# A row-wise NaN-ignoring maximum on one core: every second load of the middle tiles issued from ScalarE's queue instead of SyncE's

## The chip, the core and the metric

The kernel runs on one core of a Trainium2 chip. A core has engines with instruction streams of their own. Four of them take part here: ScalarE (ACT), GpSimd (POOL), VectorE (DVE) and SyncE (SP). SP only issues transfers. The transfers themselves are carried out by 16 DMA engines, which move data between the device's main memory (HBM) and the core's on-chip memory (SBUF, 128 partitions). An engine that issues a load does not wait for it; the load raises a semaphore when it has landed, and whoever needs the data waits on that.

The metric is the device time of one execution in microseconds (us), as the median over the runs shown.

## The reference

The input is a float32 array of 32 x 2048 x 2048. About a tenth of its elements are NaN. The result is the maximum of each row of 2048 over the elements that are not NaN:

```python
def reference(x, axis):          # axis is -1
    return np.nanmax(x, axis=axis).astype(np.float32)
```

That is 65,536 rows, 537 MB read and 0.26 MB written.

## The kernel before

**Tiles.** The rows are spread over the 128 partitions, 512 rows for each. What a partition has is cut into 74 tiles, listed in `TILES`. Lengths there are counted in quarters of a row (`Q` = 512 elements). An ordinary tile has 28 quarters, seven rows for each partition, 7,168 KB in all. An entry has three lists: how the tile is loaded, how its passes are cut, and how its reductions are cut. `([28], [7, 9, 12], [16, 12])` is one load of 28 quarters, three pieces of 7, 9 and 12 quarters, and two reductions over 16 and 12 quarters. The first tile is small; tiles 2 to 62 (counted from one) are loaded whole; the last twelve tiles come in several loads.

**Passes.** Each piece goes through three engines, all in place in the tile's buffer `xt`:
- ACT's key pass (`e_key = act(...)`) reads the upper half-word of every element and writes a 16-bit key to a buffer `kt`. The pass maps NaN below every number.
- POOL's pass turns the key back into a half-word and writes it over the upper half of the element. A negative number in the list of pieces gives that pass to ACT instead (`release()`). In five of the middle tiles, the 9th, 17th, 25th, 33rd and 41st, this is the last piece: they are cut `[9, 12, -7]`.
- DVE reduces finished stretches of the tile to row maxima (`tensor_reduce`).

ACT's third key pass of an ordinary tile also waits for POOL's first pass, since key buffers are shared.

**Buffers and order.** There are `BUFS` = 3 tile buffers. The load into a buffer waits for the last reduction of the tile that was there before, three tiles back (`free[...]`). The program is written out as one long list without loops on the chip: `Order.add` emits an instruction on an engine, puts the waits that are still needed in front of it, and returns an event for others to wait on. Each engine executes its list in order. All loads are issued by SP, in the order of the tiles, on SP's DMA queue. They use `LANES` = 14 semaphores in turn; a load also waits until the earlier one of its lane has landed.

In the profile all of ACT's passes have line 226, POOL's 236, reductions 243, and the issues of loads 307. The loop over pieces is where the change is made: `number` is already counted up there, so `number - 1` is the index, from zero, of the tile in hand.

```python
xt, before = xts[number % BUFS], free[number % BUFS]
number += 1
...
free[(number - 1) % BUFS] = after[-1:]
```

Of the kernel before, what the change touches and what calls it, by code (L numbers as in the profile page):

```python
# [10 lines left out]
Q = D // 4  # L11
# [38 lines left out]
GROUPS = [TILES[i : i + 15] for i in range(0, 60, 15)] + [TILES[60:73], TILES[73:]]  # L50
# [7 lines left out]
BUFS = 3  # L58
# [4 lines left out]
LEAD = 128  # L63

LANES = 14

# [9 lines left out]
def total(pieces):  # L78
    return sum(sum(map(abs, p)) if isinstance(p, tuple) else abs(p) for p in pieces)
# [93 lines left out]
def kernel(  # L173
# [15 lines left out]
    nc = tc.nc  # L189
    P = nc.NUM_PARTITIONS  # L190
# [9 lines left out]
    xr = x.bitcast(i32).flatten_outer_dims()  # L200
    R = xr.shape[0]
    of = out.bitcast(i32).flatten_outer_dims().rearrange("r c -> (r c)")
    rows = [sum(sum(loads) for loads, _, _ in g) * Q // D for g in GROUPS]
# [9 lines left out]
    xts = [sing.tile([P, WIDE * D], i32, name=f"xt{i}") for i in range(BUFS)]  # L213
# [5 lines left out]
    with tc.tile_critical():  # L219
        order = Order(nc)  # L220
# [51 lines left out]
        free = [[] for _ in range(BUFS)]  # L272
# [3 lines left out]
        def last(uses):  # L276

            return list({back: e for back, _, e in sorted(uses, key=lambda u: u[1])}.values())

        key = 0  # L280
        used = KEYS
        number = 0
        lanes = [[] for _ in range(LANES)]
        turn = 0
        stores = []
# [2 lines left out]
        r0 = 0  # L288
        for gi, (s, g) in enumerate(zip(rows, GROUPS)):
            xg = xr[r0 : r0 + P * s].rearrange("(p s) d -> p (s d)", p=P)  # L290
# [4 lines left out]
            base = 0  # L295
            for loads, pieces, reds in g:
                assert sum(loads) == total(pieces) == sum(reds)
                xt, before = xts[number % BUFS], free[number % BUFS]
                number += 1
                landed = []  # L300
                at = 0
                for c in loads:
                    c *= Q
                    e = order.add(
                        "sp",
                        nc.sync,
                        lambda: nc.sync.dma_start(  # L307
                            out=xt[:, at : at + c], in_=xg[:, base + at : base + at + c]
                        ),
                        before + lanes[turn],  # L310
                        lane=f"load{turn}",
                        step=16,
                    )
                    lanes[turn] = [e]
                    turn = (turn + 1) % LANES
                    landed.append((at, at + c, e))
                    at += c
                clean = []
                after = []
                at = done = 0  # L320
                reds = [n * Q for n in reds]
                part = []
                held = []
                pairs = {}
                if number not in APART:
                    pairs = joints(pieces, [n // Q for n in reds])
                flat = sum((p if isinstance(p, tuple) else (p,) for p in pieces), ())
                half = {}
                piece = 0

                def cleaned(a, b, k, i, e):

                    nonlocal clock
                    clock += 1
                    both = [(a, b, k, flat[i] < 0, clock)]
                    if i in pairs:
                        if pairs[i] not in half:
                            half[pairs[i]] = both
                            return
                        both += half.pop(pairs[i])  # L340
                    for a, b, k, back, when in both:
                        kfree[k].append((back, when, e))
                        clean.append((a, b, e))

                def name(i):
                    return f"pair{number}_{pairs[i][0]}" if i in pairs else None

                def release():
                    for a, b, k, kp, e, i in held:
                        e = act(  # L350
                            [e],
                            name(i),
                            out=xt[:, a:b].bitcast(i16)[:, 1::2],
                            in_=kp,
                            func=ACT.Copy,
                            bias=float(TOP),
                            scale=-1.0,
                        )
                        cleaned(a, b, k, i, e)
                    held.clear()  # L360

                for parts in pieces:
                    parts = parts if isinstance(parts, tuple) else (parts,)
                    c = int(sum(map(abs, parts))) * Q
                    here = [l for a, b, l in landed if a < at + c and b > at]
                    kold = []
                    if used + c > KEYS:
                        key = (key + 1) % NKEYS
                        used = 0
                        kold, kfree[key] = last(kfree[key]), []  # L370
                        assert all(k != key for q in half.values() for _, _, k, _, _ in q)
                        if at + c == sum(loads) * Q:

                            kold = kold + last(kfree[(key + 1) % NKEYS])
                    e_key = act(
                        here + kold,
                        out=kts[key][:, used : used + c],
                        in_=xt[:, at : at + c].bitcast(i16)[:, 1::2],
                        func=ACT.Prelu,
                        bias=EDGE,  # L380
                        scale=-1.0,
                        alpha=float(TOP - LOW) / (EDGE - NAN),
                    )
                    release()
                    for c in parts:
                        back, wait, c = c < 0, isinstance(c, float), int(abs(c)) * Q
                        kp = kts[key][:, used : used + c]
                        used += c
                        to = xt[:, at : at + c].bitcast(i16)[:, 1::2]
                        at += c  # L390
                        if back:
                            held.append((at - c, at, key, kp, e_key, piece))
                            if not wait or at == sum(loads) * Q:
                                release()
                        else:
                            e = pool(
                                [e_key],
                                name(piece),
                                out=to,
                                in0=kp,  # L400
                                scalar1=-1.0,
                                scalar2=float(TOP),
                                op0=ALU.mult,
                                op1=ALU.add,
                            )
                            cleaned(at - c, at, key, piece, e)
                        piece += 1
                        open_ = [h[0] for h in held] + [p[0] for q in half.values() for p in q]
                        while reds and done + reds[0] <= min([at] + open_):
                            n = reds.pop(0)  # L410


                            lo = done - 1 if done % D else done
                            done += n
                            row = (base + lo) // D
                            if done % D:
                                m, to = 1, xt[:, done - 1 : done].bitcast(f32)
                            else:
                                m = max(n // D, 1)
                                to = acc[:, row : row + m]  # L420
                            e = dve(
                                [e for a, b, e in clean if b > lo and a < done] + part,
                                nc.vector.tensor_reduce,
                                out=to,
                                in_=xt[:, lo:done]
                                .bitcast(f32)
                                .rearrange("p (c d) -> p c d", c=m),
                                axis=mybir.AxisListType.X,
                                op=ALU.max,
                            )  # L430
                            part = [e] if done % D else []
                            after.append(e)
                free[(number - 1) % BUFS] = after[-1:]
                base += at
# [16 lines left out]
        for (og, bits), e in zip(stores, ready):  # L451
# [5 lines left out]
                lane="store",  # L457
                step=16,
# [39 lines left out]
```

## Time and profile before

| what | value |
|---|---|
| median of 3 runs | 1252.92 us (1252.90 to 1252.95) |
| the profiled execution's own time | 1252.86 us |
| its span in the profile | 1251.1 us |
| DVE busy | 1110.8 us, 89% |
| ACT busy | 965.5 us, 77% |
| POOL busy | 1168.4 us, 93% |
| moved by DMA | 537.20 MB, mean 429 GB/s |

The span is what the profiler sees of the program, from its first instruction to its last; the time of the execution has a little more around it. Busy times of the engines overlap, so they do not add up. A line of the timeline has the start in the span, the duration, the engine and line, what is written from what, and in brackets how long the engine had been idle before and who released it; several instructions in a row are put together (x2), and gaps inside such a group are counted in its duration.

### The profile page before, as it was taken

How to read it: one execution, taken by the hardware profiler on the slowest of the kernel's cores; microseconds unless marked ns; L12 is line 12 of the kernel's file. 1: busy time of each engine (PE TensorE's matmuls, PEld its weight loads, DVE VectorE, ACT ScalarE, POOL GpSimd, SP SyncE). 2: the span in 40 equal slices, each digit the busy share in tenths (PEclk: the TensorE clock that was granted, in tenths of full speed). 3: DMA queues.
4: the chain of work that ended last, by engine and by line, in shares of the span. 5: the costliest groups of instructions: out<-in, count | busy, mean ns of one | idle time of the engine just before them, and what ended most of it. 6: DMA issues, size and time to landing. Idle time of an engine off the chain costs nothing.

```text
span 1251.1 us, 893 instructions
## 1 busy us (share of the span) xinstructions
DVE 1110.8 (89%) x181; ACT 965.5 (77%) x273; POOL 1168.4 (93%) x242
## 2 busy tenths in 40 slices
DVE  0888989888889888898988888998888899999999
ACT  3777887778777877788777877777777778999997
POOL 2999989998999899998999899999999999989998
DMA  9999999999999999999999999999999999999997
GB/s 415 438 416 436 440 440 436 415 440 440 438 433 420 440 440 436 433 422 440 440 436 433 422 440 438 438 433 422 440 438 437 435 422 436 427 438 428 429 428 298
DMA packets 15992, 537.20 MB, mean 429 GB/s; under 512 B 2545, under 2 KB 2545, under 8 KB 3569
## 3 DMA queue, kind: packets, MB, share of 16 engines
q1 hardware_dynamic: 15984, 537.14, 99.4%
q14 instruction: 8, 0.06, 0.0%
HBM read 536.87 MB, written 0.26 MB: 429 GB/s over the span
## 4 chain that ended last, share of the span: by engine, by line
DMA 40%; DVE 29%; POOL 22%; ACT 9%; issue 1%; SPq 0%
DMA xt<-in_x_dram 40%; DVE acc L243 29%; POOL xt L236 22%; ACT kt L226 8%; ACT xt L226 1%; SPq L307 0%; DVE none L249 0%; DVE acc L263 0%; SPq L493 0%; SPq L219 0%
## 5 line engine op out<-in xcount | busy, mean ns | idle before, releaser
L236 POOL TENSOR_SCALAR xt<-kt 128x3584 int16<-128x3584 uint16 (+11 forms) x236 | 1167.3, 4946 | 77.9 <-ACT kt L226 64.0
L243 DVE TENSOR_REDUCE acc<-xt 128x3 f32<-128x6144 f32 (+4 forms) x175 | 1107.6, 6379 | 136.6 <-POOL xt L236 129.1
L226 ACT ACTIVATE kt<-xt 128x3584 uint16<-128x3584 int16 (+9 forms) x247 | 913.3, 3734 | 278.3 <-DMA xt<-in_x_dram 258.3
L226 ACT ACTIVATE xt<-kt 128x512 int16<-128x512 uint16 (+6 forms) x24 | 52.9, 2202 | 0.7
L226 ACT ACT_TABLE_LOAD x1 | 1.3, 1283 | 0.9 <-SPq L219 0.9
L243 DVE TENSOR_REDUCE xt<-xt 128x1 f32<-128x1536 f32 x1 | 1.7, 1739 | 0.0
L269 DVE MEMSET scalars<- 128x1 f32 x1 | 0.1, 59 | 1.0 <-SPq L219 1.0
L249 DVE TENSOR_SCALAR none<-acc 128x414 int32<-128x414 f32 (+1 forms) x2 | 0.8, 381 | 0.1
L263 DVE TENSOR_TENSOR acc<-acc,none 128x414 int32<-128x414 int32 (+1 forms) x2 | 0.7, 374 | 0.1
L249 POOL TENSOR_SCALAR late<-acc 128x91 int32<-128x91 f32 x1 | 0.5, 547 | 0.1
L263 POOL TENSOR_TENSOR acc<-acc,late 128x91 int32<-128x91 int32 x1 | 0.3, 342 | 0.1
L479 POOL MEMSET const-float32-0.0<- 128x1 f32 x1 | 0.1, 98 | 0.2 <-issue 0.2
L226 ACT ACTIVATE scalars<-scalars 128x1 f32<-128x1 f32 x1 | 0.2, 203 | 0.0
L479 POOL MEMSET const-bfloat16-1.0<- 128x1 bf16 x1 | 0.1, 101 | 0.0
L479 POOL MEMSET const-uint8-127<- 128x1 uint8 x1 | 0.1, 101 | 0.0
L479 POOL MEMSET const-float32-1.0<- 128x1 f32 x1 | 0.1, 98 | 0.0
## 6 DMA issues: line engine op xcount, KB each, us to landing
xt<-in_x_dram SPq DMA_DIRECT2D x61, 7168.0 KB, 22.6
xt<-in_x_dram SPq DMA_DIRECT2D x2, 5120.0 KB, 17.5
xt<-in_x_dram SPq DMA_DIRECT2D x3, 2816.0 KB, 22.6
xt<-in_x_dram SPq DMA_DIRECT2D x4, 2048.0 KB, 22.3
xt<-in_x_dram SPq DMA_DIRECT2D x5, 1536.0 KB, 29.1
xt<-in_x_dram SPq DMA_DIRECT2D x2, 3584.0 KB, 24.7
xt<-in_x_dram SPq DMA_DIRECT2D x6, 1024.0 KB, 26.8
xt<-in_x_dram SPq DMA_DIRECT2D x3, 1792.0 KB, 30.0
```

The lines of the kernel that those rows point to most:

```text
L226: lambda: nc.scalar.activation(**kw),
L236: lambda: nc.gpsimd.tensor_scalar(**kw),
L243: return order.add("dve", nc.vector, lambda: do(**kw), deps)
L249: lambda: engine.tensor_scalar(out=none, in0=acc, scalar1=NONE, scalar2=float(0x00800000), op0=ALU.is_equal, op1=ALU.mult,),
L263: lambda: engine.tensor_tensor(out=bits, in0=bits, in1=none, op=op),
L269: e_warm = order.add("dve", nc.vector, lambda: nc.vector.memset(warm, 1.0), [])
L479: nc = _bacc.Bacc("TRN2", target_bir_lowering=False, num_devices=1)
```

## The change

A set of tiles `BESIDE` is defined: those with index 4, 6, ... 58 from zero, the 5th to the 59th, 28 in all. The load of such a tile is no longer issued by SP. ACT issues it, on ACT's own DMA queue. In ACT's list it stands two tiles earlier in the program: behind the last key pass of the tile two back (all these tiles have three key passes), and ahead of that tile's own copy by ACT where the last piece is negative. It waits for the same event as before, the last reduction of the tile that had the buffer, and in principle for the earlier load of its lane, of which ACT has three of its own. The table `places`, filled ahead of the loop, says where in the input each tile lies. When the loop comes to such a tile, it takes the event of the load already issued and gives SP nothing to issue. The loads of the other tiles, and of all from the 60th on, stay on SP.

```diff
+BESIDE = range(4, 60, 2)
+BLANES = 3
...
+        blanes = [[] for _ in range(BLANES)]
+        bturn = 0
+        ahead = {}
+        places = {}
+        at = r0 = 0
+        for s, g in zip(rows, GROUPS):
+            xg = xr[r0 : r0 + P * s].rearrange("(p s) d -> p (s d)", p=P)
+            r0 += P * s
+            base = 0
+            for loads, _, _ in g:
+                places[at] = (xg, base, sum(loads) * Q)
+                base += sum(loads) * Q
+                at += 1
...
+                if number - 1 in ahead:
+                    landed.append((0, sum(loads) * Q, ahead.pop(number - 1)))
+                    loads = []
+                size = total(pieces) * Q
                 for c in loads:
...
-                for parts in pieces:
+                for step, parts in enumerate(pieces):
...
                     release()
+                    if number + 1 in BESIDE and step == len(pieces) - 1:
+                        xa, ba, na = places[number + 1]
+                        ahead[number + 1] = order.add(
+                            "act",
+                            nc.scalar,
+                            lambda: nc.scalar.dma_start(
+                                out=xts[(number + 1) % BUFS][:, :na], in_=xa[:, ba : ba + na]
+                            ),
+                            free[(number + 1) % BUFS] + blanes[bturn],
+                            lane=f"beside{bturn}",
+                            step=16,
+                        )
+                        blanes[bturn] = [ahead[number + 1]]
+                        bturn = (bturn + 1) % BLANES
```

The remaining lines of the diff put `size` where `sum(loads) * Q` stood, since `loads` is emptied for these tiles.

More of the change, by code (lines that the diff above doesn't have):

```diff
@@ L371 @@
                         assert all(k != key for q in half.values() for _, _, k, _, _ in q)
-                        if at + c == sum(loads) * Q:
+                        if at + c == size:
                             kold = kold + last(kfree[(key + 1) % NKEYS])
@@ L392 @@
                             held.append((at - c, at, key, kp, e_key, piece))
-                            if not wait or at == sum(loads) * Q:
+                            if not wait or at == size:
                                 release()
```

## The prediction

> **What bounds the kernel now.** I read the page first, for the engines' shares and the transfers.
>
> ```profile
> DVE 1110.8 (89%) x181; ACT 965.5 (77%) x273; POOL 1168.4 (93%) x242
> DMA packets 15992, 537.20 MB, mean 429 GB/s; under 512 B 2545, under 2 KB 2545, under 8 KB 3569
> q1 hardware_dynamic: 15984, 537.14, 99.4%
> xt<-in_x_dram SPq DMA_DIRECT2D x61, 7168.0 KB, 22.6
> ```
>
> The transfers use 99.4% of what the 16 DMA engines have in the span, all on one queue; POOL, the busiest engine, has 93%. A 7,168 KB load lands 22.6 us after its issue. Next, the table by stretches (length, busy time with instruction counts of DVE, ACT and POOL, clock, DMA share, GB/s):
>
> ```profile
> 20.00:500.00 480.00, 415.96 (x55) 364.07 (x88) 451.33 (x81) 1.00 1.00 434
> 500.00:1000.00 500.00, 447.66 (x60) 378.11 (x92) 481.33 (x88) 1.00 1.00 434
> ```
>
> In the whole middle, where the change lies, the DMA share is 1.00 and the rate is 434 GB/s in both halves. At that rate one tile, 7.34 MB, takes 16.91 us. The view of the transfers in a stretch of that length shows what they are made of:
>
> ```profile
> DMA packets 144, 7.34 MB, mean 434 GB/s; under 512 B 16, under 2 KB 16, under 8 KB 16
> q1 hardware_dynamic: 144, 7.34, 100.3%
> ```
>
> 128 large packets and 16 tiny ones: for each DMA engine eight data packets of 16.91 / 8 = 2.11 us and one small closing packet. Then the waits and the timeline:
>
> ```profile
> ACT kt L226 <- DMA xt<-in_x_dram: 258.3, 69, 15.0
> SPq L307 <- DVE acc L243: 1155.7, 71, 37.8
> ```
>
> ```profile
> 78.12 6.54 DVE L243 TENSOR_REDUCE acc<-xt 128x3 f32<-128x6144 f32 x1
> 81.02 5.32 ACT L226 ACTIVATE kt<-xt 128x6144 uint16<-128x6144 int16 x1 [0.38 <-POOL xt L236]
> 84.69 17.26 SPq L307 DMA_DIRECT2D xt<-in_x_dram  x2
> 90.42 7.12 ACT L226 ACTIVATE kt<-xt 128x3584 uint16<-128x3584 int16 x2 [4.08 <-DMA xt<-in_x_dram]
> 93.69 16.74 POOL L236 TENSOR_SCALAR xt<-kt 128x3584 int16<-128x3584 uint16 x3 [0.16 <-ACT kt L226]
> 97.92 5.32 ACT L226 ACTIVATE kt<-xt 128x6144 uint16<-128x6144 int16 x1 [0.38 <-POOL xt L236]
> 103.34 15.14 DVE L243 TENSOR_REDUCE acc<-xt 128x4 f32<-128x8192 f32 x2 [1.75 <-POOL xt L236]
> 107.36 7.12 ACT L226 ACTIVATE kt<-xt 128x3584 uint16<-128x3584 int16 x2 [4.11 <-DMA xt<-in_x_dram]
> ```
>
> ACT waits about 4.1 us for data before each tile, and tiles begin at 90.42 and 107.36, 16.94 apart. SP issues at 84.69, 0.03 us after the reduction that began at 78.12 ends (84.66). The chain of waits shows the ring of three buffers:
>
> ```profile
> 67.79 22.60 DMA xt<-in_x_dram
> 90.42 3.20 ACT kt L226
> ```
>
> The next load in that chain starts at 118.51: 50.72 us later, three tiles of 16.91. Of that, 28.1 us lie between landing and release (90.42 to 118.51), and 22.6 between issue and landing. The data needs 16.9 of the 22.6. A store of 3.5 KB, alone on the queue at the end, takes 1.4 us from issue to landing, so I take 1.4 for what a load needs besides its data. That leaves 22.6 - 16.9 - 1.4 = **4.3 us that a load stands in line** behind the one before it (5.7 if nothing is taken off). This margin keeps the DMA engines busy, and it is what the change draws on.
>
> **The change part by part.** *What stays.* Bytes, passes, buffers, and what a load waits for: the load of tile i+2 still waits for the last reduction of tile i-1. The bytes at 434 GB/s set the end. So the starting sum is the profiled execution's own 1252.86 us (span 1251.1 and 1.8 around it), 0.06 under the median 1252.92.
>
> *Issuing.* 28 of the loads (tiles 5, 7, ... 59) go from SP to ACT. One issue takes SP 0.33 us (the single issue at 84.69 in SP's timeline), 28 x 0.33 = 9.2 us taken off SP, which waited 1,155.7 us for DVE anyway: 0. On ACT the 9.2 us lie in the 4.1 us that it waits before a tile: 0. Were that cover gone, 9.2. It is gone in the tiles cut 9, 12, -7 (9, 17, 25, 33, 41): there ACT's copy starts at 153.88, takes 4.20 us, and the next first pass starts at 158.06 with no wait. Up to 5 x 0.33 = 1.7 us fall on ACT there; each delays a release by 0.33 of the 4.3 us margin: 0.
>
> *The wait that ACT now has.* Behind the load on ACT stand that copy in five tiles, and else the first pass of the next tile; POOL waits for both through the keys, and DVE for POOL. The reduction waited for ends at 101.6 in the tile that begins at 90.42; its third pass runs from 97.92 to 103.24 and the next tile begins at 107.36. So the wait is over 5.8 us before ACT has anything to do; in the tile with the copy the reduction ends at 152.3, 1.6 us before the copy. 0. SP no longer waits for those reductions, but the odd loads wait for their own, a tile later: 0.
>
> *When ACT's load goes out.* Here is the first unknown. If the issue waits until the third pass is done, it stands at 103.24 instead of 101.6: **1.7 us later** per load. If it goes while that pass still runs, **0**. The nearest row: ACT's two first passes take 3.19 and 4.03 us by their shape's mean, 7.22, but 7.12 as a pair; the next instruction starts 0.1 us before its forerunner ends, so ACT's sequencer is at least one instruction ahead. I take 0 and keep 1.7.
>
> The Trainium skill's page "Perfetto Trace Analysis", section "Per-instruction lifecycle", has a rule for this: an ACT instruction is pushed into a wait queue and the sequencer is then free, while a hardware DMA is handled by the sequencer itself. By it the issue is not late at all; without it the sum would carry the 1.7 us above.
>
> *Two queues on the same DMA engines.* The second unknown. On one queue a load's packets all go behind those of the load before. On two, they can alternate. When ACT's load arrives, the older one has 4.3 us left, two packets per engine; alternating lets new packets in between. If one data packet slips in, the older load lands 2.1 us later; if another precedes its closing packet, 4.2. No byte is lost: those packets are done early. But a later landing is a later release, and the margin of 4.3 is drawn down to 2.2 or 0.1. That still suffices: at 0.1 the engines run dry for a moment only where something else is late too. Lower end 0; upper end one packet, 2.1 us, lost once when the order of landings settles, since idle time itself restores the phase. I take the middle, **1.1 us**.
>
> The row that shows queues mixing: two 8 KB instruction fetches on their own queue fall inside the load that lands at 259.97, and that landing is 17.34 us after the one before instead of 16.91. A fetch gets in ahead of data already queued, at 0.43 us for the pair. At 434 / 16 = 27.1 GB/s per engine one fetch is 0.30; what remains, 0.13, is the most that switching there and back cost, and if both hit the slowest engine (0.60) the switch cost nothing. With two switches on 55 loads the upper end is 110 x 0.13 = 14 us, the lower 0; I take 0, since the fetch's own bytes explain most of it.
>
> The Trainium skill's page "DMA: Bandwidth & Descriptors", section "Queues, rings and completion order", speaks against the change: each DMA engine takes turns between the queues that have work, a packet at a time. By that rule the older load does land late and the sum has the 1.1 us; by a strict first-come order it has 0.
>
> Sum: 1252.86 + 0 (issue) + 0 (wait) + 0 (late issue) + 1.1 + 0 (switching) = **1254.0 us**.
>
> **The rivals.** (a) *ACT issues late, and alternation leaves no margin* (slower). Late by 1.7, with two packets let in (4.2): 1.7 + 4.2 - 4.3 = 1.6 us short for each of 28 loads, 45 us at most. With nothing let in, 1.7 is under 4.3 and the loss is 0. Middle 23 us: 1276. It decides from 0.1 us of lateness with two packets let in, from 2.2 us with one. For it: the diff puts the load behind a 5.3 us pass. Against it: the 0.1 us overlap.
>
> (b) *Alternation alone is too much where the margin is smallest* (slower). From the 49th tile the pieces change; the view of the transfers there has 22.4 us from issue to landing, and 21.8 for tile 59: margins of 4.1 to 3.5, 0.1 to 0.7 short of two packets. About ten loads, up to 5 us in total beyond the 1.1, with some switching price on top up to 9: 1255.5 to 1262, say 1258.
>
> (c) *Two queues fill the DMA engines better* (faster). The page's slices show up to 440 GB/s against 434. At 440 a tile takes 16.68; then POOL's 16.74 us per tile binds: (16.91 - 16.74) x 55 = 9.4 us, 1243.5. Against it: the slices count whole packets, and the DMA share of 1.00 leaves no gap to fill. It needs only 2.5 us, 0.05 per load, to count.
>
> (d) *The second queue changes nothing*, since loads still go out one at a time and are served in that order: 1252.9.
>
> **How the numbers follow.** A no-change result is within 0.2%, 2.5 us: 1250.4 to 1255.4, about what a measurement of this kernel can tell. Chances: my forecast 0.33 and (d) 0.17, together 0.50 for the same; (a) 0.26 and (b) 0.18, 0.44 slower; (c) 0.06 faster. My forecast and (d) alone span 1252 to 1255.4. The range leaves out (c) and, above, the worse part of (a), where more than 27 of its 45 us come about (about 0.10): 1251.5 to 1280.
>
> **What the changed profile would show.** Step "issue": 28 loads under ACT's queue, 33 of that size left under SP's, about 0.33 us each. Step "late issue": ACT's load follows the reduction's end by 0.03 us, not the third pass's end. Step "two queues": SP's tiles land later or unevenly, ACT's first passes no longer 16.9 apart but alternating by a packet of 2.1; loads of both queues in one stretch. Step "switching": still 434 GB/s at a share of 1.00 in the middle. ACT's wait before a tile stays near 4 us. I am wrong if the share falls under 1.00 between loads (a, b), or if the rate rises (c).

## The result

| kernel | median | range |
|---|---|---|
| before | 1252.93 us | 1252.90 to 1252.97 |
| after | 1268.88 us | 1267.91 to 1269.66 |

The changed kernel is slower by 16.0 us; the ratio is 1.0127, 95% interval 1.0109 to 1.0144. The profiled execution took 1269.66 us with a span of 1267.9, 16.8 us over the span before.

The page of the changed kernel, its transfers (queue, packets, MB, share; then issues with size and time to landing):

```profile
DMA packets 15992, 537.21 MB, mean 424 GB/s; under 512 B 2544, under 2 KB 2544, under 8 KB 3568
q1 hardware_dynamic: 11952, 331.62, 61.3%
q10 hardware_dynamic: 4032, 205.52, 37.9%
xt<-in_x_dram SPq DMA_DIRECT2D x33, 7168.0 KB, 23.2
xt<-in_x_dram ACTq DMA_DIRECT2D x28, 7168.0 KB, 23.3
```

The change does what it says: 28 loads have moved to a second queue, q10. The number and size of packets are as before. The two queues together still fill 99.2% of a span that is longer. So the DMA engines are no less busy, and yet they move less. The table by stretches says where (columns as in the prediction):

```profile
20.00:500.00 480.00, 409.36 (x55) 360.83 (x87) 444.69 (x81) 1.00 1.00 429
500.00:1000.00 500.00, 439.07 (x58) 368.82 (x89) 471.03 (x85) 1.00 1.00 425
```

The share is 1.00 in both halves, and the rate is 429 and 425 GB/s where it was 434. A busy share is time in which a packet is under way; it does not show that packets have become longer. In the list of waits (total, times, longest), POOL's share in ACT's waiting has grown, from 19.1 to 50.2 us, and the wait for data has become a little less (258.3 us before, in the prediction). The first line is of the kernel before, the other two of the changed kernel:

```profile
ACT kt L226 <- POOL xt L236: 19.1, 51, 0.8
```

```profile
ACT kt L230 <- DMA xt<-in_x_dram: 242.8, 70, 15.0
ACT kt L230 <- POOL xt L240: 50.2, 56, 2.5
```

The timeline of the changed kernel near the start of the change:

```profile
80.14 6.54 DVE L247 TENSOR_REDUCE acc<-xt 128x3 f32<-128x6144 f32 x1
83.01 5.32 ACT L230 ACTIVATE kt<-xt 128x6144 uint16<-128x6144 int16 x1 [0.37 <-POOL xt L240]
86.71 0.33 ACTq L411 DMA_DIRECT2D xt<-in_x_dram  x1
90.32 7.12 ACT L230 ACTIVATE kt<-xt 128x3584 uint16<-128x3584 int16 x2 [1.99 <-DMA xt<-in_x_dram]
107.23 7.12 ACT L230 ACTIVATE kt<-xt 128x3584 uint16<-128x3584 int16 x2 [2.08 <-DMA xt<-in_x_dram]
126.79 7.12 ACT L230 ACTIVATE kt<-xt 128x3584 uint16<-128x3584 int16 x2 [4.84 <-DMA xt<-in_x_dram]
143.67 9.26 ACT L230 ACTIVATE kt<-xt 128x4608 uint16<-128x4608 int16 x2 [4.07 <-DMA xt<-in_x_dram]
```

Two things are to be seen. ACT's load goes out at 86.71, 0.03 us after the reduction ends (80.14 + 6.54 = 86.68), while the third pass runs until 88.33: the issue is not late. And tiles no longer begin at an even pace: 16.91 us apart, then 19.56, then 16.88. A packet takes 2.1 us, and landings now come about one packet early or late.

The packet records of the two traces give the rest. I call the time from a load's issue to the mean start of its first packets on the 16 engines its **lead**. Counted over the loads of the 5th to the 59th tile:

```text
                                             before   after
lead, mean us                                  4.72    2.92
closing packet after the last data packet
  has ended, slowest engine, mean us           0.34    1.78
loads where that is over 1 us                     0      38   of 55
large packets beyond their 2.116 us,
  whole run, us for each DMA engine            0.15   13.55
DMA engines idle up to the 62nd tile,
  us for each                                  0.26    3.25
```

The last two rows account for the loss: 13.4 us of longer packets and 3.0 us of idle time make 16.4 of the 16.8 us. Most of the lengthening, 11.5 us of it, is in the first of a load's eight packets: about 2315 ns on SP's queue and 2295 on ACT's instead of 2116; the second packet takes about 2143 and 2128, the others at most 2124.

The packets also show what the two queues do to each other. In none of the 55 loads did a data packet of the newer load go ahead of a data packet of the older one, on any engine, though the newer load had been issued 2.9 us before its turn on average. What is overtaken is the closing packet alone, by one data packet of the newer load. And the 1.8 us by which the lead fell come from two things: some 1.4 us are the later closing packet of the tile three back, whose buffer the load takes, and some 0.5 us a longer time from landing to release (28.10 us before, 28.63 after), for a tile that lands on time behind a late one has to wait for the engines.

There were two explanations for the slow first packets. *The change of queue costs*: whenever a DMA engine turns from one queue to the other, the first packet is slow. *The lead costs*: a closing packet that waits behind a packet of the other queue makes the landing late, so the release is late, so a later load reaches the engines too shortly before its turn, and a load that comes so late starts slowly. The loads whose tile three back landed over 1 us late had 2.6 us between issue and turn, the others 3.5.

### The profile page after: what moved, and what is told of

The parts are those of the page before. It is cut to its first block, busy times and chain, and to the rows that moved or that the text cites. A ratio compares the mean times of both kernels' runs of the same rounds, so it can differ in the third digit from the quotient of the medians.

```text
span 1267.9 us, 893 instructions
## 1 busy us (share of the span) xinstructions
DVE 1110.7 (88%) x181; ACT 965.6 (76%) x273; POOL 1168.3 (92%) x242
## 3 DMA queue, kind: packets, MB, share of 16 engines
q10 hardware_dynamic: 4032, 205.52, 37.9%
## 4 chain that ended last, share of the span: by engine, by line
DMA 40%; POOL 26%; DVE 21%; ACT 12%; issue 1%; SPq 0%
DMA xt<-in_x_dram 40%; POOL xt L240 26%; DVE acc L247 21%; ACT kt L230 11%; ACT xt L230 1%; DVE xt L247 0%; SPq L328 0%; DVE none L253 0%; DVE acc L267 0%; SPq L528 0%; SPq L223 0%
```

## Experiments

### Fewer changes of queue

```diff
-BESIDE = range(4, 60, 2)
+BESIDE = range(4, 60)                                  # all on ACT
+BESIDE = [n for n in range(4, 60) if n // 2 % 2 == 0]  # pairs
+BESIDE = range(4, 60, 4)                               # every fourth
```

These are three kernels, each with one of the added lines. All on ACT:

> All 56 loads of the 5th to the 60th tile are issued by ACT in the same way, so that consecutive loads are again on one queue; it changes only twice. If every change of queue between two loads costs the 0.29 us that the changed kernel lost per change (16.0 us over 56 changes), this takes 1253 to 1254 us. If issuing from ACT costs, whatever the queue before, the loss doubles with twice the loads: 1285 us. If the ring's margin is lost because ACT's issue comes late, it doubles too.

Pairs:

> 28 loads on ACT as in the changed kernel, but in pairs (5th and 6th tile, 9th and 10th, ... 57th and 58th), so that the queue changes at 28 places instead of 56. Cost per change of queue: 1252.9 + 28 x 0.29 = 1261 us. Cost per load on ACT: 1269 us as in the changed kernel. Ring margin alone (late landings that no longer fit): under 1256, since a landing between two loads of one queue gives the margin back.

Every fourth:

> Only every fourth tile's load (5th, 9th, ... 57th: 14 loads) on ACT; 28 changes of queue. Cost per change: 1261 us, the same as with the pairs. Cost per load on ACT: 1261 too, so that only the pairs tell these two apart. Ring margin alone: under 1256.

| kernel | loads on ACT | changes of queue | ratio to before (95%) | median us | over before |
|---|---|---|---|---|---|
| after | 28 | 56 | 1.0127 (1.0109 to 1.0144) | 1268.88 | 16.0 |
| all on ACT | 56 | 2 | 1.0013 (1.0003 to 1.0023) | 1254.59 | 1.7 |
| pairs | 28 | 28 | 1.0100 (1.0085 to 1.0116) | 1264.84 | 11.9 |
| every fourth | 14 | 28 | 1.0110 (1.0091 to 1.0128) | 1266.16 | 13.2 |

With all loads on ACT the middle is as before; its table by stretches:

```profile
20.00:500.00 480.00, 415.70 (x55) 363.70 (x88) 451.15 (x81) 1.00 1.00 433
500.00:1000.00 500.00, 447.93 (x60) 378.33 (x92) 481.23 (x88) 1.00 1.00 435
```

So issuing from ACT costs next to nothing, and what costs is the alternation. (A price per change would have given 1253 to 1254 us here, and it took 1254.6.) But that price is not constant: 0.29 us with 56 changes, 0.43 and 0.47 with 28. Pairs and every fourth came out at none of the values named ahead: half the changes did not halve the loss (1261), it did not vanish (under 1256), and the pairs did not cost as much as the changed kernel (1269). The packet records of the kernel with every fourth load show why "per change" is the wrong count. Of its SP loads that followed another SP load, 20 had a lead under 3 us, and their first packets took 0.21 us more, though no queue had changed; 5 loads with a lead of 2.5 to 3 us behind a change took 0.24 more.

For all on ACT, the profiled execution's span is 2.0 us over that before, and 0.5 of it is there when the 62nd tile has been read. The rest comes after that, where the loads are SP's again; its cause is open.

### A visit to another queue, by itself

```diff
-                if number - 1 in ahead:
-                    landed.append((0, sum(loads) * Q, ahead.pop(number - 1)))
-                    loads = []
...
-                                out=xts[(number + 1) % BUFS][:, :na], in_=xa[:, ba : ba + na]
+                                out=scalars[:, 8 + 8 * bturn : 16 + 8 * bturn].bitcast(i32), in_=xa[:, ba : ba + 8]
```

All tile loads stay on SP, and the end of the program waits for the small loads (those lines are not shown).

> All tile loads on SP as before the change; at each of the 28 places ACT issues a load of 32 bytes per partition into unused columns, whose completion nobody waits for until the end. If the engines pay at any change to another queue that has work, 28 visits with a change each way cost as much as the changed kernel: 1269 us. If they pay only when a large load of one queue follows a large load of the other, or when the closing packet of one waits for the other: within 2 us of 1253.

It took 1255.02 us, ratio 1.0016 (1.0007 to 1.0026): 2.1 us. The page's queues:

```profile
q1 hardware_dynamic: 15984, 537.14, 99.2%
q10 hardware_dynamic: 4032, 0.12, 0.2%
```

4,032 packets are 252 on each DMA engine, and each lasts 9 ns by the record: 252 x 9 ns = 2.3 us, which is about the whole difference. Large packets took no longer (0.12 us in all for each engine), and the mean lead is 4.69. Going to another queue for such small packets and coming back shows no price beyond the packets fetched there.

### A larger margin

```diff
-                                .rearrange("p (c d) -> p c d", c=m),
+                                .rearrange("p (c d) -> p c d", c=m)[
+                                    :, :, : Q if 4 <= number <= 58 and not reds else None
+                                ],
```

The release then comes sooner. On the kernel before:

> The kernel before, with the last reduction of the 4th to the 58th tile reading only the first quarter of each row (the maxima of those rows are left out in part). Releases come some 4.7 us sooner, so the margin in line grows from 4.3 to about 9 us. Every theory: the loads still set the end, 1252.5 to 1253.5 us. It is the yardstick for the next run.

On the changed kernel:

> The changed kernel with the same shortened reductions (the same maxima left out in part). The queue still changes 56 times and closing packets can still be late, but the margin is about 9 us. If the loss comes from loads that reach the DMA engines too shortly before their turn, it is gone: within 2 us of the yardstick. If the engines pay for the change of queue itself, it stays: 16 us over the yardstick, 1269.

The yardstick took 1252.90 us (ratio 1.0000, 0.9991 to 1.0010). Its mean lead is 9.79 us, and packets last as long as before (0.21 us longer in all, against 0.15): more lead than 4.7 brings nothing. The changed kernel took 1277.57 us, ratio 1.0192 (1.0175 to 1.0209), so the loss grew to 24.7. That speaks against both expectations, but the margin was not what I had meant it to be. Its timeline:

```profile
188.82 16.75 POOL L240 TENSOR_SCALAR xt<-kt 128x3584 int16<-128x3584 uint16 x3 [5.70 <-ACT kt L230]
193.05 5.32 ACT L230 ACTIVATE kt<-xt 128x6144 uint16<-128x6144 int16 x1 [0.37 <-POOL xt L240]
193.05 0.33 ACTq L411 DMA_DIRECT2D xt<-in_x_dram  x1
```

The load goes out at 193.05, exactly when the third pass starts; the reduction that it waits for had ended 6.64 us before (at 186.41). ACT's issue does not need the pass ahead of it to end, but it does not overtake a pass that has not started either. With releases moved forward, ACT's place in the order became the bound for 24 of its 28 loads, which went out at the start of that pass, most of them 1 to 7.5 us late, and only SP's loads had more margin. The packets say the same: the first packets of those 24 took 2484 ns on average, SP's 2117. Both kinds stand behind a change of queue.

So the next kernel puts ACT's load one pass earlier.

```diff
-                    if number + 1 in BESIDE and step == len(pieces) - 1:
+                    if number + 1 in BESIDE and step == len(pieces) - 2:
```

> As the changed kernel with shortened reductions, but ACT's load stands behind the second key pass of the tile two back, not the third, so that ACT no longer reaches it after the release (there it did so 1 to 7 us late) and the larger margin of about 9 us holds for both queues. The same maxima are left out in part. The queue changes 56 times. If only the time between issue and turn counts, it is at least 4 us everywhere, and the time is within 2 us of the yardstick's 1252.9. If alternating queues cost something by themselves, 1260 or more. If landings late by packets of the other queue eat any margin, however large, also 1260 or more.

It took 1256.69 us, ratio 1.0036 (1.0021 to 1.0051). The loss fell from 24.7 to 3.8 us, with the same 56 changes of queue; the middle is back at the rate before:

```profile
20.00:500.00 480.00, 280.21 (x55) 361.05 (x88) 444.15 (x81) 1.00 1.00 433
500.00:1000.00 500.00, 299.18 (x60) 376.39 (x92) 482.34 (x88) 1.00 1.00 435
```

Closing packets are late in 54 of its 55 landings, more than in any other kernel, and the lead of the 5th to the 59th tile is 3.95 us on average, 2.6 at least: late landings are harmless as long as the lead stays. They do take margin, though: the yardstick's mean lead was 9.79 us, and the expectation had counted on at least 4 us everywhere. What is left is more than the 2 us expected. About 2.4 of the 3.9 us of span are there by the end of the 62nd tile's data: first packets 0.28 us longer in the 6th tile, where the alternation begins, 0.83 longer in the 62nd, which had a lead of 1.1 us after the return to one queue, and 1.1 us more of idle time than before make most of it. The rest lies behind that; its cause is open.

### One queue, issue made late

The reverse: the kernel before, with only SP's queue, whose loads are held back.

```diff
+        third = {}
...
-                        before + lanes[turn],
+                        before + lanes[turn] + (third[number - 3] if 4 <= number - 1 < 60 else []),
...
                     release()
+                    third[number - 1] = [e_key]
```

> The kernel before, all loads on SP's queue, but the loads of the 5th to the 60th tile also wait for the third key pass of the tile two back: 1.7 us later. One queue, no change of it. If the loss is a matter of the time between issue and turn, that time falls from 4.7 to about 3.1 us, where first packets of the changed kernel took about 0.1 us more: 56 x 0.1, 1256 to 1261 us. If a change of queue is needed, 1253, as the margin of 4.3 us of the prediction also says.

And with two short passes more, which SP waits for in place of the key pass:

```diff
+    junk = flag.tile([P, 512], f32, name="junk")
...
+                    if 2 <= number - 1 < 58 and at + c == sum(loads) * Q and flat[-1] > 0:
+                        for _ in range(2):
+                            third[number - 1] = [
+                                act(third[number - 1], out=junk, in_=kts[key][:, used : used + 512], func=ACT.Copy)
+                            ]
```

> As the last, with two short extra passes on ACT (0.6 us each, into unused columns, in ACT's idle time before the next tile) that the loads also wait for: about 3 us later than before, except in the five tiles whose last piece is ACT's. Time between issue and turn about 2 us; first packets of the changed kernel with 2 to 2.5 us took 0.35 us more. With that delay lengthening the ring again, about 0.3 us x 51: 1264 to 1273 us. If a change of queue is needed: 1253.

The first took 1258.38 us (1255.27 to 1260.25), ratio 1.0038 (1.0023 to 1.0053): 5.5 us slower with one queue and an issue 1.7 us later. Its timeline:

```profile
81.03 5.32 ACT L226 ACTIVATE kt<-xt 128x6144 uint16<-128x6144 int16 x1 [0.37 <-POOL xt L236]
86.38 0.33 SPq L308 DMA_DIRECT2D xt<-in_x_dram  x1
90.79 7.12 ACT L226 ACTIVATE kt<-xt 128x3584 uint16<-128x3584 int16 x2 [4.45 <-DMA xt<-in_x_dram]
```

The load goes out when the pass ends, at 86.35, and the tile that lands next is there at 90.79. By the prediction's arithmetic 1.7 us of a margin of 4.3 would have cost nothing. The profiled execution is one of the quicker ones, 1255.45 us, so its trace shows less than half of the median's loss.

The second took 1297.51 us, ratio 1.0357 (1.0337 to 1.0378): 44.7 us, where 11 to 20 were expected. Its DMA share is no longer 1.00:

```profile
20.00:500.00 480.00, 393.91 (x52) 375.11 (x128) 427.42 (x77) 1.00 0.98 412
500.00:1000.00 500.00, 430.64 (x57) 389.80 (x142) 462.08 (x84) 1.00 0.99 416
```

The delay there is not a constant 3 us: most issues came 3 to 6 us after the release. The likely reason is a feedback that the expectation priced too low: the extra passes follow key passes, which follow a landing, so a late landing makes them later still. No run separates it. Here, with a single queue, large packets took 30.7 us more for each engine, and the engines were idle for 16.5.

### All kernels together

Each loss in the span against what the packet records show for each DMA engine (large packets; idle up to the 62nd tile; lead and late closings over the 5th to the 59th):

```text
kernel             span over   longer    idle   mean   late
                   before us   packets   us     lead   closings
before                   0.0      0.15    0.26   4.72     0
short before             0.0      0.21    0.27   9.79     0
all on ACT               2.0      0.45    0.30   4.53     0
small loads beside       2.1      0.12    0.26   4.69     0
issue 1.7 us late        2.6      2.30    0.78   3.29     0
short, ACT earlier       3.9      1.45    1.36   3.95    54
pairs                   11.3      9.00    2.39   3.24    12
every fourth            13.0     10.09    2.57   3.06    27
after                   16.8     13.55    3.25   2.92    38
short after             26.2     11.81   13.27   3.53    38
issue later still       46.6     30.72   16.45   2.26     1
```

And every load of the 5th to the 59th tile, of all eleven kernels, sorted by its lead and by whether its queue is that of the load before:

```text
lead us      same queue                  other queue
             loads  first packet longer  loads  first packet longer
under 2         16      572 ns              10      667 ns
2.0 to 2.5      31      326                 23      346
2.5 to 3.0      33      214                 34      254
3.0 to 3.5      60       58                 66       58
3.5 to 4.0      29       12                 33       13
over 4         214        0                 56        1
```

At an equal lead the change of queue makes little difference, and over 3 us none. What decides is the lead, and the two kernels on one queue show that it is a cause and not only a companion: only the issue was moved, and the packets lengthened. Why a load with a short lead starts slowly is not shown by these traces; they only show that it takes 3.5 to 4 us of lead here until nothing is lost. One more observation has the same size: in the two shortened kernels with two queues, some loads did get data packets in ahead of the older load's data, and on no engine did such a packet start sooner than 3.4 us after its issue.

## Why the prediction was right or wrong

**The bound: right.** The transfers set the end. In most kernels the span grew by what packets lengthened and engines idled, within 0.8 us. Exceptions are the small loads, whose packets are themselves the cost, and all on ACT and the two shortened kernels with two queues, where 1.5 to 1.7 us lie elsewhere.

**"Issuing", "The wait that ACT now has", "When ACT's load goes out": right, all 0.** Issues take 0.33 us on ACT. The cover is another than the prediction named: in the changed kernel every one of the 28 falls inside a running pass of ACT, not in its wait for data. The load leaves 0.03 us after the reduction. All 56 loads on ACT cost 1.7 us, and most of that not in the middle. The shortened kernel shows the limit of the step: the issue waits for the start of the pass ahead.

The Trainium skill's page "Perfetto Trace Analysis", section "Per-instruction lifecycle", says that the sequencer is free once an ACT instruction is in the wait queue. The trace agrees that the issue falls inside a running pass (86.71, in a pass from 83.01 to 88.33), but it does not show it passing one that still waits (193.05 for both in the shortened kernel).

**"Two queues", the mechanism: right in part.** Closing packets do stand behind a packet of the other queue, landings come about 2.1 us late, tiles begin 19.6 and 14.8 apart, and the margin is drawn down by it: the closing packet's mean delay grew by 1.44 us and the lead fell by 1.8. But new data packets do not get in between the older load's data packets, as the prediction had it: that happened in none of the 55 loads.

The Trainium skill's page "DMA: Bandwidth & Descriptors", section "Queues, rings and completion order", has the engines taking turns between queues a packet at a time. The late closing packets agree with it in 38 of 55 landings, not in all. The data packets of the changed kernel do not: both queues had work for 2.9 us on average, and the older load's data always went first. In the two shortened kernels newer data did go ahead on all 16 engines, where the load was issued over 8 us before the end of the older one's data.

**"Two queues", the size: this step failed.** The prediction said that the margin of 4.3 us could be used up to 0.1 us, that this "still suffices", and that the loss is at most one packet, once; its middle, 1.1 us, gave the sum of 1254.0. Measured were 16.4 us for this term, 1268.9 in all. The margin was taken as time that can be spent free of charge until the engines run dry. It can't: the price begins at a lead below some 4 us, 58 ns on the first packet at 3.0 to 3.5 and 572 and more below 2, and it is paid by every load anew. Idle engines, the loss that the prediction looked for, are the smaller part, 3.0 us. For the same reason its sign of being wrong would have missed the loss: it named a share under 1.00 or a higher rate, and the share stayed at 1.00 while the rate fell to 429 and 425 GB/s. No row of the kernel before could show this, since its shortest lead among these loads is 3.8 us. That it was only one profile at one margin should have widened the upper end of this term, instead of closing it at one packet.

**"Switching": right at 0.** The small loads cost about what their packets last, 2.3 us against 2.1 measured, and 56 loads behind a change with more than 4 us of lead lost 1 ns.

**The rivals.** (a) has the time's order of size (1276) but needs a late issue, which did not happen. (b) is nearest in kind, a margin too small; it was put at the last ten loads alone and priced at 1258, but it held from the eighth tile on. (c) did not happen: the rate fell. (d) is refuted by the late closings. By the prediction's own bound of 2.5 us for no change, "same" with 0.50 was the wrong side, and the change is slower by 16.0. That the measured time lies within the range is luck: the range reached so high only for (a), whose late issue did not happen.

## What to carry to other kernels

A transfer queue that is always full can still move less: look at how long single packets last and how long before its turn each load is issued, not only at the busy share. Keep the loads of a transfer-bound loop on one queue, whichever engine issues them, or make sure that each is issued well ahead (here 4 us) even when its predecessor lands a packet late. A margin read from one profile says how far things can move before an engine is idle, not how far they can move for free; holding the issue back by a known time on the old kernel measures that directly.

## What was not expected of the hardware

- The first packets of a load last longer the less time lies between its issue and its turn: 0 at over 4 us, 58 ns at 3.0 to 3.5, 214 to 254 at 2.5 to 3.0, 572 to 667 under 2, of a packet that otherwise lasts 2116 ns. In the changed kernel the DMA share reads 1.00 while this goes on.
- Two queues with work cost nothing by themselves: 433 and 435 GB/s with 56 changes of queue at a mean lead of 3.95 us.
- With two queues at work and a lead of about 3 us, data packets kept the order in which their loads were issued, in all 55 loads; only closing packets were overtaken, in 38.
- ACT issues a load while the pass ahead of it is running (28 of 28 in the changed kernel), but not before that pass has started (24 of 28 in the shortened one).
